# The lead of a hybrid decoder layer: rows normalized before they are turned, bias and norm weight taken into the modulation's dot products, all weight blocks split in two, and filler passes on TensorE

## The chip, the cores and the metric

One core of a Trainium2 chip runs one launch of the kernel. The metric is the device time of a launch in microseconds. The engines are named as the profile names them: PE is TensorE's matmul (PEld its weight load), DVE is VectorE, ACT is ScalarE, POOL is GpSimd, SP is SyncE, which issues nearly all the loads from memory.

## The reference, cut to what matters

One decoder layer on 256 tokens of width 1024 (FFN width 2816), in float32:

```python
def rmsnorm(x, g):
    return x * lax.rsqrt(jnp.mean(x * x, -1, keepdims=True) + EPS) * g

mod = silu(c) @ w_ada + b_ada                       # 9 rows of 1024
sh1, sc1, g1, sh2, sc2, g2, sh3, sc3, g3 = jnp.split(mod, 9, axis=-1)
u = rmsnorm(h, norm_ff1) * (1 + sc1) + sh1
h = h + 0.5 * g1 * ((silu(u @ w_gate) * (u @ w_up)) @ w_down)
u = rmsnorm(h, norm_mix) * (1 + sc2) + sh2
h = h + g2 * token_mixing(u, ...)
u = rmsnorm(h, norm_ff2) * (1 + sc3) + sh3
h = h + 0.5 * g3 * swiglu(u, ...)
return rmsnorm(h, norm_final)
```

The change touches only the start: the first two lines of the first FFN (its modulation, its norm, and the first 8 of its 22 gate and up column blocks).

## The kernel before, in words

Activations stand feature-major: a tile holds 128 features on the partitions and 256 tokens along the row, and the width of 1024 is 8 such blocks k = 0..7. Float32 weights are multiplied in three passes: ACT copies a block of weights to a rounded part (`hi`), DVE subtracts it from the original to get the rest (`lo`), the activations `u` are parted in the same way (`uh`, `ul`), and PE adds hi·uh, hi·ul and lo·uh, 128x128 weights against 128x256 activations each time.

The **lead** is the kernel's first stage. Its 8 PSUM banks hold gate and up of the FFN's column blocks f = 0..7, 16 results of 128x256, and k runs in the outer loop, so that PE can begin when the first eighth of the weights is there. For each k the stage needs: the two dot products that give scale and shift of this block (`lead_dot`, letter d: a row of `w_ada` for each of the 128 features times silu(c), with `accum_out`), the sums with bias and norm weight (`lead_mods`, m), the normed block (`lead_normed`, n: x times 1/rms, which PE has spread over all partitions into `rb`), the modulated block `u` (`lead_u`, u, on ACT), its parts `uh` (`lead_uh`, c, ACT) and `ul` (`lead_ul`, v, DVE), and the weights' hi (`lead_high`, h, ACT) and lo (`lead_low`, r, DVE), in two pieces i = 0, 1. Of the 16 weight blocks, 14 are split; two (`NATIVE`) are multiplied unsplit in float32 (`lead_native`, p). `lead_mm` (x) issues the passes of one piece.

What stands in which order is written by hand: the string `LEADING` lists these steps by letter, k and piece, and `InOrder` chains each instruction of DVE, ACT and PE behind the one recorded before it on its engine. An engine therefore issues in the order of the string, and waits where its next instruction has to wait. `LOADS` gives the order of the loads on SP (a for `w_ada`, l for the weights, each in two pieces); they go into 4 buffers `raw`, so that a load of block k waits until a buffer of block k-2 has been read.

Behind the lead, `LED` finishes its 8 banks (silu, product, split), then the loop over `work1` runs the other gate/up blocks and the down projection of the first FFN, with the remaining dot products of the modulation between them (`AdaQueue`), then token mixing, then the second FFN and the last norm.

`h`, the residual in feature-major order, is made at the start: PE transposes x through `ident` into 4 banks, ACT copies them to `h` (`take_in`).

Of the kernel before, what the change touches and what calls it, by code (L numbers as in the profile page):

```python
# [77 lines left out]
def hybrid_layer(ctx: ExitStack, tc: tile.TileContext, x, cols, ident_d, tri_d, mask_d, onehot_d,  # L78
                 relT, wlr, ada, lead, gu1, dn1, win, gv, mv, gbr, wout, gu2, dn2, out):
# [90 lines left out]
    def split(raw, lo, width=1024, later=False, gap=False):  # L170
# [124 lines left out]
    for s in (1, 4, 7):  # L295
# [44 lines left out]
    class AdaQueue:  # L340
# [255 lines left out]
    def lead_dot(k, i):  # L596

        lead_load_until(f"a{k}{i}")
        ada_dot(ada_raw[k], 0 if i else D, 0 if i else 1, k)

    def lead_mods(k):
        vec.scalar_tensor_tensor(mods[:, 1, k:k + 1], gemv[:, 1, k:k + 1], bada[:, 1, k:k + 1],
                                 colt[:, C_N1 + k:C_N1 + k + 1], op0=ALU.add, op1=ALU.mult)
        vec.tensor_tensor(out=mods[:, 0, k:k + 1], in0=gemv[:, 0, k:k + 1], in1=bada[:, 0, k:k + 1], op=ALU.add)


    def lead_normed(k):
        if k:
            vec.tensor_tensor(out=xn[:, k, :S], in0=h[:, k, :S], in1=lead_rb[0][:, :S], op=ALU.mult)
        else:  # L610
            vec.scalar_tensor_tensor(xn[:, 0, :S], h[:, 0, :S], mods[:, 1, 0:1], rb[:, :S], op0=ALU.mult, op1=ALU.mult)

    def lead_u(k):
        us[k] = row(tag="u", bufs=3)
        act.activation(us[k], xn[:, k, :S], AF.Identity, scale=mods[:, 1, k:k + 1] if k else 1.0, bias=mods[:, 0, k:k + 1])

    def lead_uh(k):
        if k:
            act.activation(uh[:, k, :S], us[k], AF.Copy)
        else:  # L620
            act.activation(uh[:, 0, :S], xn[:, 0, :S], AF.Identity, bias=mods[:, 0, 0:1])

    def lead_ul(k):
        if k:
            vec.tensor_tensor(out=ul[:, k, :S], in0=us[k], in1=uh[:, k, :S], op=ALU.subtract)
        else:
            vec.scalar_tensor_tensor(ul[:, 0, :S], xn[:, 0, :S], mods[:, 0, 0:1], uh[:, 0, :S], op0=ALU.add,
                                     op1=ALU.subtract)
# [10 lines left out]
    def lead_native(k):  # L639
        for i in range(NATIVE):  # L640
            b = lead_banks[i // 2]
            mm(b[:, i % 2 * S:(i % 2 + 1) * S], b, lead_raw[k][:, blk(i)], us[k], stop=(k == KD - 1))

    def lead_mm(k, w):
        def to(at):
            i = NATIVE + w * half + at
            return lead_banks[i // 2][:, i % 2 * S:(i % 2 + 1) * S], lead_banks[i // 2]

        if k or w:
            for at in range(half):  # L650
                mm3(*to(at), ws[k, w], blk(at), (uh[:, k, :S], ul[:, k, :S]), stop=(k == KD - 1))
        else:

            for part, rows in ((0, uh), (1, uh), (0, ul)):
                for at in range(half):
                    mm(*to(at), ws[0, 0][part][:, blk(at)], rows[:, 0, :S])

    def lead_rbs():
        act.activation(rbs, rb[:, :S], AF.Copy)
        lead_rb[0] = rbs  # L660
# [40 lines left out]
    warm_bank = bank()
    for _ in range(WARM):
        ten.transpose(warm_bank[:, :P], ident, ident)
    ada_dot(ada_raw[0], D, 1, 0)
    ada_dot(ada_raw[0], 0, 0, 0)
    rbs, lead_rb = row(tag="rbs", bufs=1), [rb]
# [19 lines left out]
    def mix_constants():  # L726
        ctri = load(tri_d, 1536)
# [505 lines left out]
def _packed(i):  # L1233
    w = {k: np.asarray(v) for k, v in i.items()}
    d = {}
    d["x"] = _c(w["x"][0])
    vec = [w["b_ada"][0], w["norm_ff1"][0], w["norm_mix"][0], w["norm_ff2"][0], w["norm_final"], w["c"][0],
# [6 lines left out]
    first = rows[:2].transpose(1, 2, 0, 3).reshape(KD, P, 2 * D)  # L1244
# [44 lines left out]
```

## Time and profile before

| | us |
|---|---|
| median of 3 runs | 572.95 (572.29 to 573.03) |
| the profiled execution, its own time | 572.64 |
| its span on the core | 570.9 |
| PE busy | 557.3 (98%) |
| DVE busy | 442.8 (78%) |
| ACT busy | 300.8 (53%) |
| DMA queue of SP, share of 16 engines | 67.6% |

The profile is one execution. The page's first part gives the busy time of each engine over the whole span; windows give the same for any stretch, with PE's granted clock (1.00 is the higher of its two levels, 0.50 the lower) and what the DMA engines moved. A timeline lists instructions by start and duration, with the idle time before one and what ended it in square brackets. Instructions of DVE and ACT overlap a little at their ends, so what one costs in a row of them is the distance between two starts, and not its duration.

### The profile page before, as it was taken

To read this page: it belongs to the slowest core of one execution; us is meant where nothing else is said; L and a number is where in the kernel's file an instruction comes from. 1 tells how busy PE (TensorE), PEld (TensorE's weight loads), DVE (VectorE), ACT (ScalarE), POOL (GpSimd) and SP (SyncE) were. 2 spreads that over 40 slices of the span, in tenths; PEclk is the share of its full clock that TensorE was granted. 3 is DMA by queue.
4 is the path that set the end of the run, shared out by engine and by line. 5 is a ranking of instruction groups with operands and counts; after the bars stand their busy time and mean duration, and the time that the engine had idled before them with its cause. 6 is when DMAs were issued, how large, how long until landed. Compare 5 with 4: busy or idle time off the path is not lost.

```text
span 570.9 us, 11312 instructions
## 1 busy us (share of the span) xinstructions
PE 557.3 (98%) x4711; PEld 550.1 (96%) x4711; DVE 442.8 (78%) x701; ACT 300.8 (53%) x480; POOL 10.8 (2%) x14
## 2 busy tenths in 40 slices
PE   4999999999999999999999999999999999999996
PEld 3999999999999999998999999999999999999995
DVE  4999887879887896899998979789874656665534
ACT  5455664352536577843764544576644454345424
POOL 0000000000000010000001000001000000000000
PEclk9999999999999999999999999999999999999999
DMA  8999689898989726544489776842796566775102
GB/s 311 357 409 394 255 314 383 302 359 325 325 313 338 242 75 249 193 140 157 130 307 365 287 265 251 309 152 84 284 342 205 195 212 205 254 266 180 67 1 75
DMA packets 23237, 140.95 MB, mean 247 GB/s; under 512 B 2781, under 2 KB 3346, under 8 KB 8850
## 3 DMA queue, kind: packets, MB, share of 16 engines
q1 hardware_dynamic: 22722, 139.37, 67.6%
q8 instruction: 37, 0.61, 0.4%
q0 software_dynamic: 176, 0.53, 0.3%
q10 hardware_dynamic: 288, 0.33, 0.2%
q14 instruction: 14, 0.11, 0.1%
HBM read 139.16 MB, written 1.05 MB: 246 GB/s over the span
## 4 chain that ended last, share of the span: by engine, by line
PE 61%; issue 32%; DVE 4%; DMA 2%; SPq 0%; POOL 0%; ACT 0%; POOLq 0%; DVEq 0%
PE b L103 61%; DMA raw<-in_lead 2%; DVE b L103 1%; DVE lo L103 1%; DVE s L103 1%; DVE raw L103 0%; POOL tiny L363 0%; ACT hi L103 0%; SPq L579 0%; SPq L276 0%; POOLq L1284 0%; DVEq L1284 0%; ACT ub L103 0%; SPq L273 0%; DVE tiny L103 0%
## 5 line engine op out<-in xcount | busy, mean ns | idle before, releaser
L103 PE MATMUL b<-ub,hi 128*128 128x256 f32 (+1 forms) x1888 | 329.3, 279 | 3.2 <-ACT ub L103 3.2
L103 PEld LDWEIGHTS b<-ub,hi 128*128 128x128 f32 x1888 | 286.6, 189 | 5.1 <-ACT ub L103 3.4
L103 DVE TENSOR_TENSOR lo<-raw,hi 128x1024 fp32r<-128x1024 f32 (+2 forms) x188 | 223.2, 1211 | 66.6 <-ACT hi L103 65.1
L103 PE MATMUL b<-ub,lo 128*128 128x256 f32 (+1 forms) x944 | 261.1, 278 | 0.0
L103 ACT ACTIVATE hi<-raw 128x1024 fp32r<-128x1024 f32 (+2 forms) x188 | 191.5, 1044 | 83.4 <-issue 34.4
L103 PEld LDWEIGHTS b<-ub,lo 128*128 128x128 f32 x944 | 177.6, 189 | 0.0
L103 PE MATMUL b<-s,hi 128*128 128x256 f32 x960 | 165.4, 277 | 0.0
L103 PEld LDWEIGHTS b<-s,hi 128*128 128x128 f32 x960 | 144.8, 188 | 0.0
L103 PE MATMUL b<-s,lo 128*128 128x256 f32 x480 | 132.7, 277 | 0.0
L103 PEld LDWEIGHTS b<-s,lo 128*128 128x128 f32 x480 | 90.1, 188 | 0.0
L103 DVE SCALAR_TENSOR_TENSOR raw<-raw,cact 128x1024 f32<-128x1024 f32 x72 | 85.0, 1219 | 2.5 <-DMA raw<-in_ada 2.2
L103 ACT ACTIVATE s<-m 128x256 fp32r<-128x256 f32 x52 | 21.4, 417 | 76.7 <-DVE m L103 76.7
L103 ACT ACTIVATE sg<-b 128x256 f32<-128x256 f32 x46 | 17.0, 379 | 44.9 <-PE b L103 42.9
L103 DVE TENSOR_TENSOR s<-m,s 128x256 fp32r<-128x256 f32 x52 | 21.8, 424 | 20.6 <-ACT s L103 20.5
L103 DVE TENSOR_TENSOR m<-sg,b 128x256 f32<-128x256 f32 x43 | 17.8, 416 | 12.5 <-ACT sg L103 12.2
L103 ACT ACTIVATE s<-b 128x256 f32<-128x256 f32 (+5 forms) x33 | 13.9, 469 | 22.0 <-PE b L103 19.6
L103 PE MATMUL b<-hi,ub 128*128 128x264 f32 (+1 forms) x96 | 21.8, 321 | 0.0
L103 PEld LDWEIGHTS b<-hi,ub 128*128 128x128 f32 x96 | 15.8, 188 | 1.2
L103 PE MATMUL b<-lo,ub 128*128 128x264 f32 (+1 forms) x48 | 15.4, 321 | 0.0
L103 DVE SCALAR_TENSOR_TENSOR b<-b,mods,b 128x256 f32<-128x256 f32 x25 | 11.0, 477 | 4.7 <-PE b L103 4.6
L363 POOL TENSOR_TENSOR tiny<-tiny,mhalf 128x2 f32<-128x2 f32 (+1 forms) x5 | 7.1, 1418 | 365.5 <-DVE tiny L103 365.5
L103 ACT ACTIVATE sq<-b 128x256 f32<-128x256 f32 x24 | 9.2, 407 | 5.6 <-DVE b L103 5.2
(122 smaller groups left out, 276.4 us busy)
## 6 DMA issues: line engine op xcount, KB each, us to landing
raw<-in_gu SPq DMA_DIRECT2D x35, 1024.0 KB, 5.3
raw<-in_ada SPq DMA_DIRECT2D x28, 1024.0 KB, 6.1
raw<-in_dn SPq DMA_DIRECT2D x21, 1024.0 KB, 4.9
raw<-in_win SPq DMA_DIRECT2D x12, 1024.0 KB, 6.4
raw<-in_ada SPq DMA_DIRECT2D x16, 512.0 KB, 7.4
raw<-in_gbr SPq DMA_DIRECT2D x8, 1024.0 KB, 7.2
raw<-in_lead SPq DMA_DIRECT2D x8, 576.0 KB, 6.3
raw<-in_wout SPq DMA_DIRECT2D x4, 1024.0 KB, 5.9
```

The costliest lines, as they stand in the source:

```text
L103: x = getattr(self.engine, op)(*args, **kw)
L363: nc.gpsimd.tensor_tensor(out=rs[:, :n], in0=ms[:, :n], in1=mhalf[:, :n], op=ALU.pow)
```

## The change

- **Rows.** The sum of squares of the second 128 tokens is shared between ACT and DVE. Then 1/rms scales the rows of x in place while they are token-major (`lead_scaled`, s, ACT, in four halves), PE transposes the scaled rows (`lead_turned`, t) and ACT copies the banks to `xn` (`lead_xn`, e). `lead_normed`, `rb` and `rbs` go, and so does `lead_rbs`.
- **Dot products.** A row of `w_ada` comes with two more columns, the bias and 1 (scale) or 0 (shift); `cact` has two columns of 1 behind silu(c); the scale's dot product is multiplied by the norm weight. So `gemv` holds norm weight times (1 + scale), and the shift, at once. `lead_mods` goes. The rows of these loads are 4104 bytes long and contiguous (`adal`), where they were 4096 of 8192.
- **Blocks.** All 16 weight blocks are split: two pieces of 1024 columns, and `lead_native` goes. The passes of a piece go over the banks in another order (`IN_TURN`). The first piece of k = 0 is split in two halves on ACT and DVE.
- **Order.** `LEADING` has `v` (ul) directly behind the dot products and in front of `r` (lo of piece 0).
- **Filler passes.** `keep_warm` has PE transpose `ident` into a spare bank: 22 passes after silu(c) has been turned, 8 and 7 between and behind the transposes of x (5 before).
- **Residual.** `h` is no longer made from x at the start but loaded from a second, feature-major copy `xT` in `mix_constants`, 1 MB on SP's queue.

```diff
-WARM = 5
+WARM = (22, 8, 7)
...
-LEADING = """h00 m0 n0 c0 r00 v0 u0 b t n1 h01 r01 h10 d10 d11 m1 u1 c1 r10 v1 n2 h11 r11 x00 x01 p0 h20 d20 d21 m2
-         u2 c2 r20 v2 n3 h21 r21 p1 x10 x11 h30 d30 d31 m3 u3 c3 r30 v3 n4 h31 r31 p2 x20 x21 h40
...
+LEADING = """u0 c0 h00 e1 v0 r00 h01 e2 e3 d10 r01 d11 h10 u1 c1 v1 r10 h11 r11 x00 x01 h20 d20 d21 u2 c2 v2 r20 h21 r21
+             x10 x11 h30 d30 d31 u3 c3 v3 r30 h31 r31 x20 x21 h40 d40 d41 u4 c4 v4 r40 h41 r41 x30 x31
...
+        parts = [(src, to_hi, to_lo)]
+        if pieces == 2:
+            parts = [(src[:, i], to_hi[:, i], to_lo[:, i]) for i in range(2)]
...
-    cact = cst.tile([P, D], F32, name="cact")
+    cact = cst.tile([P, D + 64], F32, name="cact")[:, :D + 2]
+    vec.memset(cact[:, D:], 1.0)
...
+    warm = bank()
+
+    def keep_warm(n):
+
+        for _ in range(n):
+            ten.transpose(warm[:, :P], ident, ident)
+
+    keep_warm(WARM[0])
...
-    vec.scalar_tensor_tensor(sq[1], xt[:, D:2 * D], 1.0, xt[:, D:2 * D], op0=ALU.mult, op1=ALU.mult,
-                             accum_out=ssq[:, 1:2])
+    act.activation(sq[1][:, 0:512], xt[:, D:D + 512], AF.Square, accum_out=ssq[:, 1:2])
+    vec.scalar_tensor_tensor(sq[1][:, 512:], xt[:, D + 512:2 * D], 1.0, xt[:, D + 512:2 * D], op0=ALU.mult,
+                             op1=ALU.mult, accum_out=ssq[:, 2:3])
+    vec.tensor_tensor(out=ssq[:, 1:2], in0=ssq[:, 1:2], in1=ssq[:, 2:3], op=ALU.add)
...
     def lead_dot(k, i):
 
         lead_load_until(f"a{k}{i}")
-        ada_dot(ada_raw[k], 0 if i else D, 0 if i else 1, k)
-
-    def lead_mods(k):
...
+        src = ada_raw[k][:, 2 * GV * i:2 * GV * i + D + 2]
+        vec.scalar_tensor_tensor(src, src, 1.0 if i else colt[:, C_N1 + k:C_N1 + k + 1], cact, op0=ALU.mult,
+                                 op1=ALU.mult, accum_out=gemv[:, 1 - i, k:k + 1])
 
     def lead_u(k):
         us[k] = row(tag="u", bufs=3)
-        act.activation(us[k], xn[:, k, :S], AF.Identity, scale=mods[:, 1, k:k + 1] if k else 1.0, bias=mods[:, 0, k:k + 1])
+        if k:
+            act.activation(us[k], xn[:, k, :S], AF.Identity, scale=gemv[:, 1, k:k + 1], bias=gemv[:, 0, k:k + 1])
+        else:
+            vec.tensor_scalar(us[0], xn[:, 0, :S], gemv[:, 1, 0:1], gemv[:, 0, 0:1], op0=ALU.mult, op1=ALU.add)
...
     def lead_high(k, i):
         lead_load_until(f"l{k}{i}")
-        ws[k, i], rests[k, i] = split(lead_raw[k], (NATIVE + i * half) * P, half * P, True)
+        ws[k, i], rests[k, i] = split(lead_raw[k], i * D, later=True, gap=True, pieces=1 if k or i else 2)
...
+        rows, both = (uh, ul), range(KD)
+        order = [(at, *p) for at in IN_TURN for p in ((0, 0), (0, 1), (1, 0))]
+        if k == 0:
+            halves = (both,) if w else (range(4), range(4, 8))
+            order = [(at, 0, r) for part in halves for r in (0, 1) for at in part] + [(at, 1, 0) for at in both]
...
-    rb, _ = spread(rs, range(2))
...
+    def lead_scaled(t, half):
+        sl = slice(t * D + half * 512, t * D + (half + 1) * 512)
+        act.activation(xt[:, sl], xt[:, sl], AF.Copy, scale=rs[:, t:t + 1])
...
+    lead_dot(0, 0)
+    lead_dot(0, 1)
+    play("s00 t00 s10 t10 s01 w1 e0 s11 t01 t11 w2", {
+        "s": lead_scaled, "t": lead_turned, "e": lead_xn, "w": lambda i: keep_warm(WARM[i])})
...
+        nc.sync.dma_start(h.rearrange("p k s -> p (k s)"), xT)
...
+    more = np.zeros((2, KD, P, 2), np.float32)
+    more[:, :, :, 0] = w["b_ada"][0].reshape(9, KD, P)[:2]
+    more[1, :, :, 1] = 1.0
+    d["adal"] = _c(np.concatenate([rows[:2], more], 3)[::-1].transpose(1, 0, 2, 3))
```

In the rows that follow, a name stands for a tile (out <- in, then the shape): `raw` with `gemv` is a dot product, `mods` a sum with bias, `lo` a weight rest, `ub` the parts of the activations (here `ul`), `b_12`/`b_9` is `xn`, `tiny` the sums of squares.

DVE, block k = 2, before: seven rows from the dot products on.

```order
L103 SCALAR_TENSOR_TENSOR raw_253,gemv<-raw_253,cact 128x1024 x2
L103 SCALAR_TENSOR_TENSOR mods<-gemv,bada,colt 128x1
L103 TENSOR_TENSOR mods<-gemv,bada 128x1
L103 TENSOR_TENSOR lo_259<-raw_256,hi_258 128x896
L103 TENSOR_TENSOR ub_137<-u_265,ub_137 128x256
L103 TENSOR_TENSOR b_12_136<-b_7_112,rbs_165 128x256
L103 TENSOR_TENSOR lo_273<-raw_256,hi_272 128x896
```

The same in the changed kernel, with the next block's first row:

```order
L101 SCALAR_TENSOR_TENSOR raw_285,gemv<-raw_285,colt,cact 128x1026
L101 SCALAR_TENSOR_TENSOR raw_285,gemv<-raw_285,cact 128x1026
L101 TENSOR_TENSOR ub_75<-u_295,ub_75 128x256
L101 TENSOR_TENSOR lo_291<-raw_288,hi_290 128x2x512
L101 TENSOR_TENSOR lo_302<-raw_288,hi_301 128x2x512
L101 SCALAR_TENSOR_TENSOR raw_353,gemv<-raw_353,colt,cact 128x1026
```

The two `mods` rows and the normed block are gone, and `ub` has moved from behind the first `lo` to in front of it.

DVE, blocks 0 and 1, before:

```order
L103 SCALAR_TENSOR_TENSOR raw_138,gemv<-raw_138,cact 128x1024 x2
L103 SCALAR_TENSOR_TENSOR mods<-gemv,bada,colt 128x1
L103 TENSOR_TENSOR mods<-gemv,bada 128x1
L103 SCALAR_TENSOR_TENSOR b_12_136<-b_7_112,mods,b_154 128x256
L103 TENSOR_TENSOR lo_175<-raw_141,hi_174 128x896
L103 SCALAR_TENSOR_TENSOR ub_137<-b_12_136,mods,ub_137 128x256
L103 TENSOR_TENSOR b_12_136<-b_7_112,rbs_165 128x256
L103 TENSOR_TENSOR lo_189<-raw_141,hi_188 128x896
L103 SCALAR_TENSOR_TENSOR raw_144,gemv<-raw_144,cact 128x1024 x2
L103 SCALAR_TENSOR_TENSOR mods<-gemv,bada,colt 128x1
L103 TENSOR_TENSOR mods<-gemv,bada 128x1
L103 TENSOR_TENSOR lo_193<-raw_147,hi_192 128x896
```

and in the changed kernel:

```order
L101 SCALAR_TENSOR_TENSOR raw_139,gemv<-raw_139,colt,cact 128x1026
L101 SCALAR_TENSOR_TENSOR raw_139,gemv<-raw_139,cact 128x1026
L101 TENSOR_SCALAR u_206<-b_9_138,gemv 128x256
L101 TENSOR_TENSOR ub_75<-u_206,ub_75 128x256
L101 TENSOR_TENSOR lo_210<-raw_142,hi_209 128x512 x2
L101 SCALAR_TENSOR_TENSOR raw_145,gemv<-raw_145,colt,cact 128x1026
L101 TENSOR_TENSOR lo_218<-raw_142,hi_217 128x2x512
L101 SCALAR_TENSOR_TENSOR raw_145,gemv<-raw_145,cact 128x1026
L101 TENSOR_TENSOR ub_75<-u_228,ub_75 128x256
L101 TENSOR_TENSOR lo_226<-raw_148,hi_225 128x2x512
L101 TENSOR_TENSOR lo_234<-raw_148,hi_233 128x2x512
```

The dot products of block 1 now stand on both sides of the last `lo` of block 0, and in block 1 too `ub` stands ahead of both `lo`.

PE at the start, before (`csil` is silu(c), `b_1_72` is x, `tiny` is 1/rms being spread; a row with `ident` alone is filler):

```order
L103 MATMUL b_95<-ident,csil 128x128 x4
L103 MATMUL b_96<-ident,csil 128x128 x4
L103 MATMUL b_113<-ident,b_1_72 128x128 x2
L103 MATMUL b_114<-ident,b_1_72 128x128 x2
L103 MATMUL b_115<-ident,b_1_72 128x128 x2
L103 MATMUL b_116<-ident,b_1_72 128x128 x2
L103 MATMUL b_113<-ident,b_1_72 128x128 x2
L103 MATMUL b_114<-ident,b_1_72 128x128 x2
L103 MATMUL b_115<-ident,b_1_72 128x128 x2
L103 MATMUL b_116<-ident,b_1_72 128x128 x2
L103 MATMUL b_154<-ident,tiny_152 128x128 x2
L103 MATMUL b_157<-ident 128x128 x5
```

and in the changed kernel:

```order
L101 MATMUL b_96<-ident,csil 128x128 x4
L101 MATMUL b_97<-ident,csil 128x128 x4
L101 MATMUL b_106<-ident 128x128 x22
L101 MATMUL b_155<-ident,b_1_72 128x128 x2
L101 MATMUL b_156<-ident,b_1_72 128x128 x2
L101 MATMUL b_155<-ident,b_1_72 128x128 x2
L101 MATMUL b_156<-ident,b_1_72 128x128 x2
L101 MATMUL b_106<-ident 128x128 x8
L101 MATMUL b_158<-ident,b_1_72 128x128 x2
L101 MATMUL b_159<-ident,b_1_72 128x128 x2
L101 MATMUL b_158<-ident,b_1_72 128x128 x2
L101 MATMUL b_159<-ident,b_1_72 128x128 x2
```

The transposes of x have moved behind 22 filler passes and wait for the scaled rows; 8 and (behind the last row shown) 7 more filler passes stand between them and the first weights.

## Rows read from the trace of the kernel before

**Rows 1.** The page's first part: busy time, share of the span, instructions.

```profile
PE 557.3 (98%) x4711; PEld 550.1 (96%) x4711; DVE 442.8 (78%) x701; ACT 300.8 (53%) x480; POOL 10.8 (2%) x14
```

**Rows 2.** Windows: us, PE, PEld, DVE, ACT, POOL busy, clock, DMA share, GB/s.

```profile
60.00:560.00 500.00, 499.83 (x4270) 494.61 (x4269) 389.08 (x595) 263.71 (x420) 9.10 (x7) 1.00 0.66 235
```

**Rows 3.** Chain that ended last, 0 to 70 us: start, us, what.

```profile
12.79 0.41 ACT ub L103
...
13.24 56.82 PE b L103 x455
```

**Rows 4.** Windows of PE alone: us, busy (records), granted clock, DMA share, GB/s.

```profile
6.60:7.10 0.50, 0.50 (x7) 1.00 0.93 254
10.00:13.20 3.20, 0.05 (x1) 1.00 1.02 415
13.50:16.50 3.00, 3.00 (x16) 0.50 1.03 418
```

**Rows 5.** Timeline of PE: start, us, line, operation, tiles, shape, count.

```profile
26.92 0.58 PE L103 MATMUL b<-ub,hi 128*128 128x256 f32 x2
...
55.06 0.58 PE L103 MATMUL b<-ub,hi 128*128 128x256 f32 x2
...
55.59 0.39 PE L103 MATMUL b<-ub,hi 128*128 128x256 f32 x2
...
59.67 0.39 PE L103 MATMUL b<-ub,hi 128*128 128x256 f32 x2
```

**Rows 6.** Timeline of DVE, block 2 of the lead.

```profile
21.77 1.22 DVE L103 SCALAR_TENSOR_TENSOR raw<-raw,cact 128x1024 f32<-128x1024 f32 x1
...
22.91 1.22 DVE L103 SCALAR_TENSOR_TENSOR raw<-raw,cact 128x1024 f32<-128x1024 f32 x1
24.06 0.08 DVE L103 DVE_READ_ACCUMULATOR raw<-raw,cact 128x1 f32 x1
...
24.19 0.15 DVE L103 TENSOR_TENSOR mods<-gemv,bada 128x1 f32<-128x1 f32 x1
24.26 1.08 DVE L103 TENSOR_TENSOR lo<-raw,hi 128x896 fp32r<-128x896 f32 x1
25.47 0.43 DVE L103 TENSOR_TENSOR ub<-u,ub 128x256 fp32r<-128x256 f32 x1
25.81 0.42 DVE L103 TENSOR_TENSOR b<-b,rbs 128x256 f32<-128x256 f32 x1
...
27.32 1.22 DVE L103 SCALAR_TENSOR_TENSOR raw<-raw,cact 128x1024 f32<-128x1024 f32 x1
```

**Rows 7.** Timeline of ACT, the same stretch.

```profile
24.38 0.60 ACT L103 ACTIVATE u<-b,mods 128x256 f32<-128x256 f32 x1 [0.66 <-DVE mods L103]
25.01 0.42 ACT L103 ACTIVATE ub<-u 128x256 fp32r<-128x256 f32 x1
```

**Rows 8.** Groups by form, DVE: busy us, mean ns of one, idle before.

```profile
L103 DVE TENSOR_TENSOR lo<-raw,hi 128x1024 fp32r<-128x1024 f32 x168 | 201.0, 1222 | 64.6 <-ACT hi L103 63.6 <-PE b L103 0.8
...
L103 DVE SCALAR_TENSOR_TENSOR b<-b,mods,b 128x256 f32<-128x256 f32 x25 | 11.0, 477 | 4.7 <-PE b L103 4.6
...
L103 DVE TENSOR_TENSOR s<-s,s 128x512 fp32r<-128x512 f32 x2 | 1.4, 692 | 1.4 <-ACT s L103 1.4
```

**Rows 9.** Groups by form, ACT.

```profile
L103 ACT ACTIVATE wide<-wide 128x512 f32<-128x512 f32 x2 | 1.3, 633 | 0.0
```

**Rows 10.** Timeline of DVE and ACT at the start of the lead.

```profile
10.39 1.23 DVE L103 SCALAR_TENSOR_TENSOR raw<-raw,cact 128x1024 f32<-128x1024 f32 x1
11.54 0.08 DVE L103 DVE_READ_ACCUMULATOR raw<-raw,cact 128x1 f32 x1
...
11.84 0.95 ACT L103 ACTIVATE hi<-raw 128x896 fp32r<-128x896 f32 x1 [2.96 <-DMA raw<-in_lead]
...
16.97 0.96 ACT L103 ACTIVATE hi<-raw 128x896 fp32r<-128x896 f32 x1 [1.79 <-DMA raw<-in_lead]
```

**Rows 11.** Timeline of DVE at the lead's end.

```profile
54.10 3.36 DVE L103 TENSOR_TENSOR lo<-raw,hi 128x896 fp32r<-128x896 f32 x3 [0.42 <-ACT hi L103]
```

More of the change, by code (lines that the diff above doesn't have):

```diff
@@ L168, in load, with split @@
         return t
-    def split(raw, lo, width=1024, later=False, gap=False):
+    def split(raw, lo, width=1024, later=False, gap=False, pieces=1):
         hi = wp.tile([P, 2 * GV], F32R, tag="hi", name=name("hi"), bufs=HL)
@@ L350, in step @@
                 s, q = self.todo.pop(0)
-                raw = load(ada[4 * s + q])
+                raw = load(ada[4 * (s - 2) + q])
                 ada_dot(raw, 0, s, 2 * q)
@@ L620, in lead_uh @@
         else:
-            act.activation(uh[:, 0, :S], xn[:, 0, :S], AF.Identity, bias=mods[:, 0, 0:1])
+            act.activation(uh[:, 0, :S], xn[:, 0, :S], AF.Identity, scale=gemv[:, 1, 0:1], bias=gemv[:, 0, 0:1])
     def lead_ul(k):
[L624 to L628, printed above, removed]
+        vec.tensor_tensor(out=ul[:, k, :S], in0=us[k], in1=uh[:, k, :S], op=ALU.subtract)
     rests = {}
@@ L633, in lead_high @@
         lead_load_until(f"l{k}{i}")
-        ws[k, i], rests[k, i] = split(lead_raw[k], (NATIVE + i * half) * P, half * P, True)
+        ws[k, i], rests[k, i] = split(lead_raw[k], i * D, later=True, gap=True, pieces=1 if k or i else 2)
     def lead_low(k, i):
         rests[k, i]()
[L639 to L642, printed above, removed]
     def lead_mm(k, w):
[L645 to L660, printed above, removed]
+        rows, both = (uh, ul), range(KD)
[3 more added lines that the diff above has]
+            order = [(at, 0, r) for part in halves for r in (0, 1) for at in part] + [(at, 1, 0) for at in both]
+        for at, part, r in order:
+            b = lead_banks[4 * w + at // 2]
+            mm(b[:, at % 2 * S:(at % 2 + 1) * S], b, ws[k, w][part][:, wblk(at)], rows[r][:, k, :S],
+               stop=(k == KD - 1 and part == 1))
     lead_load_until(to_load[2 * RAW - 1])
@@ L699, in hybrid_layer, with lead_turned, lead_xn @@
     rs = rstd(ssq, D, 2)
-    rb, _ = spread(rs, range(2))
[L701 to L706, printed above, removed]
+    turned_x = [bank(), bank()]
+    bank()
+    turned_x += [bank(), bank()]
+    def lead_scaled(t, half):
+        sl = slice(t * D + half * 512, t * D + (half + 1) * 512)
+        act.activation(xt[:, sl], xt[:, sl], AF.Copy, scale=rs[:, t:t + 1])
+    def lead_turned(t, half):
+        for k in range(4 * half, 4 * half + 4):
+            ten.transpose(turned_x[k // 2][:, blk(k % 2 * 2 + t)], xt[:, t * D + k * P:t * D + (k + 1) * P], ident)
+    def lead_xn(i):
+        act.activation(xn[:, 2 * i:2 * i + 2].rearrange("p k s -> p (k s)"), turned_x[i], AF.Copy)
+    lead_dot(0, 0)
+    lead_dot(0, 1)
+    play("s00 t00 s10 t10 s01 w1 e0 s11 t01 t11 w2", {
+        "s": lead_scaled, "t": lead_turned, "e": lead_xn, "w": lambda i: keep_warm(WARM[i])})
     lead_banks = [bank() for _ in range(LEAD)]
-    play(LEADING, {"d": lead_dot, "m": lead_mods, "n": lead_normed, "u": lead_u, "c": lead_uh, "v": lead_ul,
-                   "h": lead_high, "r": lead_low, "p": lead_native, "x": lead_mm, "b": lead_rbs, "t": lambda: take_in(3), "A": stream.more})
+    play(LEADING, {"d": lead_dot, "u": lead_u, "c": lead_uh, "v": lead_ul, "h": lead_high, "r": lead_low,
+                   "e": lead_xn, "x": lead_mm, "A": stream.more})
+    h = big()
     hid = Hidden()
```

57 lines of the change are left out of this document (19 added, 38 removed).

## The prediction

> **What bounds the kernel now.** I read the page's first part, then the windows, then the chain of the first 70 us. PE is busy for 557.3 of 570.9 us [rows 1], and from 60 to 560 us it is busy for 499.83 of 500 [rows 2]. So nothing behind the lead can give back time lost in the lead or swallow time won there: the prediction is the shift of the moment at which PE has done the lead's last pass. Before, that moment is 60.01: the chain is a wait for `uh`, which ACT finishes at 13.20, and then PE without a pause [rows 3]; the last group of three passes starts at 59.67, and such groups stand 0.34 apart (12 of them from 55.59 to 59.67) [rows 5]. PE pays 5.63 us for a block of the lead ((55.06 - 26.92)/5) [rows 5]. The second thing to see is DVE: its period per block is 5.55 us (21.77 to 27.32), nearly all filled [rows 6]. PE has only 0.08 us per block in hand over DVE, so the lead has two bounds that nearly tie, and an edit has to be costed on both.
>
> **PE's side of the change.** Each block loses two unsplit matmuls and gets two more groups of three. Now a block is 16 groups of 0.34, 5.44 us, against 5.63: 0.19 less per block, 1.5 us in all [rows 5]. Each pass is 0.113 us. At the start the wait for `uh` gets shorter: the last dot product is out at 11.62 [rows 10]; before, two sums, the normed block and ACT's pass followed, to 13.20 [rows 3]. Now `c0` on ACT follows at once, 0.60 long as `u` is with its two column operands [rows 7], so `uh` is there at 12.26. The first half of `hi` is there at 12.92 (below). Ahead of the first weights PE still has 4 transposes and 7 fillers, 11 records at 14 per us (7 in 0.5 us [rows 4]), 0.8 us behind the last scaled half of x, and that half stands ahead of `c0` on ACT: 11.7 + 0.8 = 12.5. So PE starts at 13.0, against 13.24. Before, the clock stood at 0.50 from 13.5 to 16.5 after PE had been idle from 10.0 to 13.2 [rows 4]; with the fillers there is no such pause. If DVE kept up, PE would run 384 passes from 13.0 on, 43.5 us, and end at 56.5, 3.5 us early. That is the most the change can bring.
>
> **DVE's side, term by term.** What is removed per block: two `mods` sums (0.20 from 24.06 + 0.08 to 24.34) and the normed block, 0.34 to 0.50 [rows 6]. What is added: 128 columns on each `lo`, so that both last 1.222 [rows 8] and start 1.15 apart, as the dot products do (22.91 to 24.06). What is moved is `ul`. Before, DVE did the first `lo` (24.26) while ACT made `u` and `uh` for it; the two took from 24.38 to 25.43, and `ul` began at 25.47 [rows 6, 7]. Now `ul` stands in front of that `lo`, directly behind the second dot product, and DVE, which issues in order, waits for ACT with both `lo` queued behind the wait. Both `lo` are what PE waits for: the third pass of a group needs the first of them. One period of DVE is then:
> - first dot product 1.15, plus 0.06 for its column operand (477 ns [rows 8] against 420 without one [rows 6]): 1.21;
> - second dot product and the reading of its sum, 1.15 + 0.08 = 1.23 [rows 6];
> - the way over ACT: 0.04 to the start of `u`, 0.63 to the start of `uh`, 0.42 for it, 0.04 back [rows 6, 7]: 1.13;
> - `ul` 0.34 (25.47 to 25.81) [rows 6];
> - two `lo`, 2 x 1.15 = 2.30.
>
> That is 6.21 us (6.15 if the column operand costs nothing), against 5.44 for PE. DVE becomes the bound of the lead; without the wait of 1.13 it would be 5.08, and PE would be the bound.
>
> **The end of the lead.** The start of DVE's chain: sum out at 11.62 [rows 10]; `c0` 11.66 to 12.26; `ul` of block 0 at 12.30, done with its slot at 12.64. ACT's first half of `hi` starts 0.63 behind `c0`, at 12.29, and lasts 0.63 [rows 9], to 12.92; two half `lo`, 0.69 long [rows 8] and 0.61 apart, end DVE's slot at 14.18. Block 1's first dot product needs its load: the weights of block 0 landed at 11.84 [rows 10], two pieces of together 0.98 MB follow in the queue, and at 415 GB/s [rows 4] they are there at 14.2. Take 14.25. Then 1.21 (dot product), 1.15 (the last `lo` of block 0), 1.23 (dot product), 1.13 (ACT), 0.34 (`ul`), 2.30 (both `lo`): block 2 starts at 21.61. For `u` of block 1 ACT must have its `hi`: that load landed at 16.97 [rows 10] and comes 64 KB earlier in the queue now, so it is no later than the sum at 17.84. Five periods of 6.21 bring block 7 to 52.66; its first `lo` is done 1.21 + 1.23 + 1.13 + 0.34 + 1.22 later, at 57.79. PE takes its third pass at 57.83 and has 46 passes from there, 5.21 us: 63.04. The shift is 63.04 - 60.01 = +3.0 us.
>
> PE itself is ready long before: at 18.4 it has done block 0 and then waits for block 1's `lo` until 20.5. So the saved passes, the earlier start and the clock are all paid back as waits, and a fall of the clock in that pause would be covered too: it cost 3.0 us at half speed before [rows 4], 1.5 us, and PE has 0.77 in hand per block from there on.
>
> **What is hidden.** The fillers and the 8 transposes lie in time in which PE waits anyway. The load of `xT`, 1.05 MB, is 2.5 us of the DMA engines at 415 GB/s [rows 4]; behind 60 us they are busy 0.66 of the time [rows 2], and it stands ahead of other loads on SP, so without that cover it costs up to 2.5 us once. `w_ada` and weights, 2.1 MB per 6.21 us, are 338 GB/s, under the 415 seen. Behind the lead DVE had its next `lo` done at 57.46 [rows 11], 2.55 us ahead of PE; now two more follow the lead's last one (58.9) and end at 61.2, 1.8 us ahead of PE's 63.04. Still ahead, so no further loss.
>
> The new load rows are 4104 bytes long. Before, the lead's loads had rows of 3584 to 4608 bytes, multiples of 512, and ran at 415 GB/s [rows 4]. The Trainium skill (DMA: Bandwidth & Descriptors, "How a descriptor splits into AXI transactions") has reads go in 256-byte transactions that start at a 256-byte boundary, so that a row which starts elsewhere fetches bytes it drops; no row here shows it. As an estimate from that page, up to 8 beats in 128 more, 6%, on four loads of 1.25 us each ahead of block 1's weights, it would add 0.3 us to the chain, and the sum would be +3.3.
>
> **Forecast.** The profiled execution took 572.64, 0.31 under the median of the runs. 572.64 + 3.0 = **575.7 us**. With the terms at their low ends (6.15, the start 0.5 earlier) it is +2.2, 574.8; with their high ends (loads 0.5 late, the median's 0.31, a clock that falls once and is not covered, 1.0) 577.5.
>
> **Rivals.**
> - *PE stays the bound, faster.* This decides as soon as DVE's period is under 5.44, that is, if the wait between the second dot product and `ul` is under 0.36 us and not 1.13. Then PE runs through from 13.0: 572.64 - 3.5 = 569.1, and 570.6 if the clock is low for the first 3.0 us all the same (1.5 us, as before [rows 4]). For it: DVE has less work than before (5.08 of 6.21). Against it: `u` and `uh` are two ACT passes of 0.60 and 0.42 in a row, both needed by `ul` [rows 7]. At 6.6 us PE ran at 14 transposes per us at a granted clock of 1.00 with nothing but transposes behind it [rows 4], so fillers seem to hold the clock. The Trainium skill (TensorE: Matmul & The Clock Gate, "Part 4: PE-mode transpose") says that transposes do not count as busy in the same way; by that rule this rival is 570.6, and not 569.1. Chance 0.10.
> - *More than DVE's wait: the clock or the loads.* If PE's pauses of 0.77 us per block let the clock fall again and again, a block takes up to 10.9 us at half speed, and even two falls of 3.0 us that are not covered cost 3 us more: 578.7. If `xT` is not hidden, 2.5 more: 578.2. Against it: before, the clock fell only behind 3.2 us without work [rows 4], four times such a pause. Chance 0.10.
> - *It does less than it says*: the wait is there but the start gains more than I count, or work behind the lead gives time back. The sum would be within 1.1 us: about 573. Rows 2 leave 0.17 us to give back. Chance 0.07.
>
> **How the numbers follow.** Forecast 0.73, with 574.8 to 577.5 as its own range. To 8 in 10 the range needs half of the two neighbours: 573.4 to 577.9. A measurement of this kernel tells about 0.2%, 1.1 us, from no change. Faster: 0.10 and a little of the third rival, 0.11. Same: 0.07. Slower: 0.82.
>
> **What would show it.** Right: in the lead DVE idles some 1.1 us per block ahead of `ub<-u,ub`, ended by ACT `ub`; its period is 6.2; PE waits about 0.8 us per block, ended by DVE `lo`, and its longest pause is in block 1; the clock is 1.00 at the first weights; work behind the lead begins near 63. Wrong: a period of DVE near 5.4 or less with no such idle time; PE without waits from 13 us on; a lead that ends before 60; waits of DVE for loads (`raw<-in_adal`) in place of ACT; PE waits behind 65 us.

## The result and the profile after

The changed kernel took 575.57 us (median of 4 runs, 575.14 to 576.67) against 572.62 (572.09 to 573.03). The ratio is 1.0055, 95% interval 1.0038 to 1.0072: slower by 2.95 us, where 575.7 was forecast. The mechanism that was forecast is in the trace. But the sum came out by luck too: two terms that the forecast did not have, +1.86 and -1.82 us, almost cancel.

The page's first part, after, against [rows 1]; columns are busy time, share of the span, instructions:

```profile
PE 558.8 (97%) x4757; PEld 551.0 (96%) x4757; DVE 439.3 (77%) x680; ACT 305.3 (53%) x485; POOL 10.8 (2%) x14
```

DVE has less work than before, and the kernel is slower. The timeline of DVE, after, block 2 of the lead (answers to [rows 6]; start, length, what; in brackets the idle time ahead and what ended it):

```profile
21.44 1.28 DVE L101 SCALAR_TENSOR_TENSOR raw<-raw,colt,cact 128x1026 f32<-128x1026 f32 x1
22.64 1.22 DVE L101 SCALAR_TENSOR_TENSOR raw<-raw,cact 128x1026 f32<-128x1026 f32 x1
23.79 0.08 DVE L101 DVE_READ_ACCUMULATOR raw<-raw,cact 128x1 f32 x1
25.00 0.42 DVE L101 TENSOR_TENSOR ub<-u,ub 128x256 fp32r<-128x256 f32 x1 [1.12 <-ACT ub L101]
25.34 2.35 DVE L101 TENSOR_TENSOR lo<-raw,hi 128x1024 fp32r<-128x1024 f32 x2
27.61 1.28 DVE L101 SCALAR_TENSOR_TENSOR raw<-raw,colt,cact 128x1026 f32<-128x1026 f32 x1
```

The period is 27.61 - 21.44 = 6.17 us (forecast 6.21, before 5.55), and 1.12 of it is the wait for ACT ahead of `ub<-u,ub`. Between the sum at 23.79 and the end of that wait ACT does this (answers to [rows 7]):

```profile
23.91 0.60 ACT L101 ACTIVATE u<-b,gemv 128x256 f32<-128x256 f32 x1 [0.58 <-DVE raw L101]
24.55 0.42 ACT L101 ACTIVATE ub<-u 128x256 fp32r<-128x256 f32 x1
```

The waits of the changed kernel, the first line from 12 to 63 us, the others of PE over the whole span (who waits, for whom, us in total, times, longest):

```profile
DVE ub L101 <- ACT ub L101: 8.5, 8, 1.1
...
PE b L101 <- DVE lo L101: 3.3, 7, 0.8
...
PE b L101 <- DMA relt<-in_relT: 1.9, 1, 1.9
```

So PE waits for `lo` in each of blocks 1 to 7; from start to start a block of the lead takes it the 6.17 us of DVE, 0.73 over its own 5.44. The third line is new, and not in the forecast. Four moments of PE give the balance. Its timeline, before, at the first pass on `s` (one unit of 48 passes, 5.44 us, behind the lead's end), at the matmul with `relt`, and at the last transposes of the program:

```profile
65.45 0.40 PE L103 MATMUL b<-s,hi 128*128 128x256 f32 x2
...
81.96 0.80 PE L103 MATMUL b<-wide,relt 32*4 32x384 f32 x2
...
563.56 1.94 PE L103 MATMUL b<-ident,b 128*128 128x128 f32 x16
```

The same three, after:

```profile
68.27 0.39 PE L101 MATMUL b<-s,hi 128*128 128x256 f32 x2
...
86.64 0.80 PE L101 MATMUL b<-wide,relt 32*4 32x384 f32 x2 [1.88 <-DMA relt<-in_relT]
...
566.42 1.94 PE L101 MATMUL b<-ident,b 128*128 128x128 f32 x16
```

The lead brings +2.82 (68.27 - 65.45; it ends at 62.83 instead of 60.01). From there to `relt` another +1.86 (86.64 - 81.96 = 4.68 in all). Then 1.82 comes back: from `relt` to the last transposes PE needs 479.78 us instead of 481.60. In all this is +2.86, as the span says (573.7 against 570.9). The middle and the last term are what the experiments had to explain, beside the first.

Where the `relt` term starts is seen on SP's queue. Before:

```profile
63.85 0.43 SPq L729 DMA_DIRECT2D mask<-in_mask  x1
...
70.63 0.41 SPq L729 DMA_DIRECT2D relt<-in_relT  x1
...
76.16 0.35 SPq L167 DMA_DIRECT2D raw<-in_tri  x1
```

After, where `xT` and `tri` stand ahead of the small loads and `tri` waits for a free `raw` buffer:

```profile
67.21 1.33 SPq L717 DMA_DIRECT2D b<-in_xT  x1
...
79.52 0.33 SPq L165 DMA_DIRECT2D raw<-in_tri  x1
...
80.84 0.42 SPq L720 DMA_DIRECT2D relt<-in_relT  x1
```

`relt` is issued 10.2 us later, with a lead that ends only 2.8 later, and lands when PE already waits for it.

### The profile page after: what moved, and what is told of

It is laid out like the page before. It is cut to its first block, busy times and chain, and to the rows that moved or that the text cites. A ratio compares the mean times of both kernels' runs of the same rounds, so it can differ in the third digit from the quotient of the medians.

```text
span 573.7 us, 11383 instructions
## 1 busy us (share of the span) xinstructions
PE 558.8 (97%) x4757; PEld 551.0 (96%) x4757; DVE 439.3 (77%) x680; ACT 305.3 (53%) x485; POOL 10.8 (2%) x14
## 4 chain that ended last, share of the span: by engine, by line
PE 52%; issue 33%; DVE 10%; ACT 2%; DMA 2%; POOL 0%; SPq 0%; DVEq 0%; POOLq 0%
PE b L101 52%; DVE lo L101 4%; DVE raw L101 3%; DVE b L101 1%; DVE s L101 1%; DMA relt<-in_relT 1%; DMA b<-in_x 1%; ACT u L101 1%; ACT ub L101 1%; ACT b L101 1%; POOL tiny L366 0%; SPq L720 0%; POOLq L1279 0%; DVEq L1279 0%; ACT hi L101 0%
## 5 line engine op out<-in xcount | busy, mean ns | idle before, releaser
L101 PE MATMUL b<-ub,lo 128*128 128x256 f32 (+1 forms) x960 | 264.0, 277 | 3.3 <-DVE lo L101 3.3
L101 DVE SCALAR_TENSOR_TENSOR raw<-raw,cact 128x1024 f32<-128x1024 f32 (+1 forms) x64 | 75.8, 1219 | 0.0
```

Source lines behind the costliest of these rows:

```text
L101: x = getattr(self.engine, op)(*args, **kw)
```

## Experiments

Times are medians; the runs of the kernel before beside each group gave 572.29 (first four), 572.55 (next four) and 572.23 us (last three).

**1. The one move, put into the kernel before.**

```diff
-h20 d20 d21 m2 u2 c2 r20 v2 n3 h21 r21
+h20 d20 d21 m2 u2 c2 v2 r20 n3 h21 r21
```

(and so in blocks 1 to 7)

> The kernel before with only the one move: in blocks 1 to 7 the low part of the rows ahead of the first lo on DVE (ub, lo, lo instead of lo, ub, lo). My theory: DVE then idles 1.1 us per block ahead of the low part, its period goes from 5.55 to about 6.2, and over 7 blocks the lead ends 3 to 4.5 us later than at 60.0; time 575.6 to 577.2. Rival (the change's loss is of its other parts: longer first stage, unaligned rows of 4104 bytes, xT): within 0.5 us of 572.6.

Measured: 576.5 us, ratio 1.0070 (1.0058 to 1.0082), +4.2. DVE's timeline of this kernel, block 2:

```profile
21.89 1.22 DVE L103 SCALAR_TENSOR_TENSOR raw<-raw,cact 128x1024 f32<-128x1024 f32 x1
...
25.59 0.43 DVE L103 TENSOR_TENSOR ub<-u,ub 128x256 fp32r<-128x256 f32 x1 [1.12 <-ACT ub L103]
...
28.27 1.22 DVE L103 SCALAR_TENSOR_TENSOR raw<-raw,cact 128x1024 f32<-128x1024 f32 x1
```

The same 1.12 us appear and the period is 6.38. Nothing else of the change is in this kernel, so the move alone is enough to make the lead late.

**2. The move taken back in the changed kernel.**

```diff
-u2 c2 v2 r20 h21 r21
+u2 c2 r20 v2 h21 r21
```

> The changed kernel with, in blocks 1 to 7, the first lo subtraction ahead of the low part of the rows again (DVE: lo, ub, lo instead of ub, lo, lo); all else as changed. My theory (DVE's wait for ACT's u and ub, 1.12 us per block, delays both lo): the wait goes, DVE's period falls from 6.17 us to about 5.2, under PE's 5.44, and PE sets the pace: 8 blocks of 5.44 from 13.1, so the lead ends near 57.0 instead of 62.7 and the time is about 570.0 us (the 1.9 us idle of PE at 84 us still there). Rival 1, the loads set the pace (2.10 MB per block; at the 350 GB/s of the changed kernel's first 60 us that is 6.0 us per block): ACT's hi waits for DMA in most blocks, lead end above 60, time 573.5 to 575. Rival 2, it is not DVE's order: no change, 575.5.

Measured: 573.7 us, ratio 1.0018 (1.0004 to 1.0031), with runs from 571.36 to 575.06: only 1.9 us less, not 5.5. The wait for `ub` is gone, but DVE's timeline of this kernel shows another:

```profile
37.10 0.42 DVE L101 TENSOR_TENSOR ub<-u,ub 128x256 fp32r<-128x256 f32 x1
38.05 1.22 DVE L101 TENSOR_TENSOR lo<-raw,hi 128x1024 fp32r<-128x1024 f32 x1 [0.52 <-ACT hi L101]
...
42.75 0.43 DVE L101 TENSOR_TENSOR ub<-u,ub 128x256 fp32r<-128x256 f32 x1
43.69 1.23 DVE L101 TENSOR_TENSOR lo<-raw,hi 128x1024 fp32r<-128x1024 f32 x1 [0.52 <-ACT hi L101]
```

ACT makes `u`, `ub`, and then the second `hi`; DVE now arrives at the second `lo` 0.52 us before that `hi` is done. The period is 43.69 - 38.05 = 5.64, still over PE's 5.44. The rival of the loads named 573.5 to 575, and the time lies in that range; but in this trace DVE waits for late weights only in block 2 (1.0 us), and kernel 4 below, with the same loads in its lead, is 4.0 us faster. PE reaches `s` at 65.42 (68.27 in the changed kernel), 2.85 earlier, with a first pass 0.5 later, since `x` landed later in this execution. So the move is worth some 3 us in the lead, and my 5.08 for DVE without its wait was short by half a microsecond. Part of the gain is lost again at `relt`: PE's row there and the windows around it (us, busy (records), granted clock, DMA share, GB/s):

```profile
83.93 0.80 PE L101 MATMUL b<-wide,relt 32*4 32x384 f32 x2 [2.03 <-DMA relt<-in_relT]
```

```profile
81.00:84.00 3.00, 0.97 (x9) 1.00 1.02 334
84.00:87.00 3.00, 3.00 (x14) 0.68 0.97 366
87.00:90.00 3.00, 3.00 (x22) 0.75 1.01 418
```

Behind this pause the granted clock was under 1.00 in the next two windows: the trace has it at 0.50, the lower level, from 85.11 to 88.52 us. In the changed kernel, behind its 1.88 us, it stayed at 1.00.

**3. The small constants ahead of `tri` and `xT`, all else as changed.**

```diff
-        nc.sync.dma_start(h.rearrange("p k s -> p (k s)"), xT)
-        ctri = load(tri_d, 1536)
         for to, src in ((mask, mask_d), (onehot, onehot_d), (relt, relT), (wlr_s, wlr)):
             nc.sync.dma_start(to, src)
+        ctri = load(tri_d, 1536)
+        nc.sync.dma_start(h.rearrange("p k s -> p (k s)"), xT)
```

> The changed kernel with the five loads of the constants in another order: mask, onehot, relt and wlr first, then tri, xT last (changed: xT, tri, mask, onehot, relt, wlr). Theory A (xT in front of the raw buffers' loads on SP's queue moved relt from 70.6 to 80.8 us, and PE stands at 84.6 for 1.88 us): the idle of PE at 84 us goes and the time falls by 1.9 us to 573.7. Theory B (the megabyte of xT itself is what delays everything, and its delay only shows elsewhere): another load lands late, the time stays within 0.7 us of 575.5.

Measured: 573.77 us, ratio 1.0024 (1.0015 to 1.0033), 1.8 less than the changed kernel. On SP `relt` is issued at 73.69, and PE's row of this kernel has no wait:

```profile
84.38 0.80 PE L101 MATMUL b<-wide,relt 32*4 32x384 f32 x2
```

Theory A holds. The megabyte of `xT` is still loaded, at 79.71, and costs nothing there: from `relt` to the last transposes PE needs 479.77 us, as in the changed kernel (479.78). So it was the order of the queue, not the bytes. The edit moves `xT` and `tri`, and in the kernel before `tri` was issued behind `relt`; which of the two held `relt` back was not separated.

**4. Both together.** Edits 2 and 3 in one kernel.

> The changed kernel with the first lo subtraction ahead of the rows' low part in blocks 1 to 7 (as lo_first) and the small constants loaded first, xT last (as small_first). If the two causes are separate, the gains add: lo_first's 1.9 us and small_first's 1.8 us, so 575.6 - 3.7 = 571.9 us. If the idle of PE at 82 us (2.3 us in lo_first, and the granted clock 0.83 in the 10 us around it) hid more of lo_first's gain, which moved the passes ahead of that idle 2.9 us forward, the time is 575.6 - 1.8 - 2.9 = 570.9 or less. If the two are one cause: 573.7.

Measured: 569.68 us, ratio 0.9949 (0.9936 to 0.9961), 2.9 faster than before and 5.9 faster than as changed. That is more than the sum of the two gains, 3.7. PE's timeline of it, at `s` and at `relt`, against 68.27 and 86.64 as changed:

```profile
64.63 0.39 PE L101 MATMUL b<-s,hi 128*128 128x256 f32 x2
...
81.04 0.48 PE L101 MATMUL b<-wide,relt 32*4 32x384 f32 x1
```

The lead is 3.64 earlier and the pause at `relt` is gone: 5.60 in all, and its span is 5.6 us shorter. So the two causes are separate, and in kernel 2 part of the first one's gain was hidden; in its one trace by the slow clock behind the longer pause, and by weights of block 2 that landed late (DVE waited 1.0 us for their `hi`, and PE passed `s` 0.8 later than here).

**5. The second term that was not foreseen: where tiles lie.** The change also takes the tile of the rows' parts (`ub`) ahead of the mid tiles, so that both lie at other addresses. That line was moved alone, first in the kernel before:

```diff
     for t in range(2):
         nc.sync.dma_start(xt[:, t * D:(t + 1) * D], x[blk(t)])
+    uh, ul = parts_tile()
...
     xn = big()
-    uh, ul = parts_tile()
```

> The kernel before with one line moved: the tile of the rows' two parts (ub, 20480 bytes per partition) is taken ahead of the mid tiles, as in the changed kernel, so that it and the mid tiles lie at other addresses of SBUF; no instruction is added, taken away or reordered on purpose. Theory A (in the trace of before some 740 passes behind the lead are 115 to 130 ns from start to start instead of 113.3, in the changed kernel 320, and the difference is one of placement): the slow passes fall to about 320 and the time by about 2.0 us to 570.6. Theory B (they come with the phase in which ACT's and DVE's instructions meet the passes): nothing changes, 572.6.

and then back, in the changed kernel (the reverse of this diff):

> The changed kernel with one line moved back: the tile of the rows' two parts is taken where the kernel before takes it, behind the mid tiles; no instruction is changed. Theory A (placement: the change won some 2 us behind the lead by moving this tile): the passes of 115 to 130 ns behind the lead rise from 324 to about 740 and the time by 1.2 (what the reverse move gave in medians) to 2.0 us, to 576.8 to 577.6. Theory B (the fewer slow passes come from something else in the change): unchanged, 575.5.

Measured: 571.05 us, ratio 0.9977 (0.9968 to 0.9986), for the kernel before; 579.1, ratio 1.0108 (1.0090 to 1.0126), for the changed one. The windows of PE from 400 to 550 us, in the order before, after, the kernel before with the tile early, the changed one with the tile late:

```profile
400.00:550.00 150.00, 150.00 (x1320) 1.00 0.60 210
```

```profile
400.00:550.00 150.00, 150.00 (x1326) 1.00 0.61 211
```

```profile
400.00:550.00 150.00, 150.00 (x1326) 1.00 0.59 206
```

```profile
400.00:550.00 150.00, 150.00 (x1320) 1.00 0.61 211
```

PE is busy all the time at full clock in all four, and does six more passes in 150 us wherever the tile is early, 0.45%. Between `relt` and the last transposes the two kernels with the early tile need 479.78 and 479.93 us, the two with the late one 481.60 and 481.73 (of the second of each pair: 81.22 to 561.15, and 86.28 to 568.01). With the traces of the other experiments, nine with the early tile need 479.77 to 479.94 us for this stretch, three with the late one 481.60 to 481.73 (the trace of experiment 2 is not among them, since its slow clock lies in the stretch). So theory A is shown for PE's pace in both directions, some 1.8 us. In the starts of single passes the late placement has some 740 and 840 passes of 115 to 130 ns behind 60 us, the early one 325 and 354; most others are 113.3. Which of the two tiles matters, and what it meets at its address, was not separated.

The times of the two kernels are less clean. The first gained 1.2 us of the 2.0 expected. In its profiled execution the span is 2.41 us shorter, but only 1.67 of this lie behind `relt`; most of the rest is in the lead, where PE's first passes begin at 12.76 us and not 13.24, and 0.113 us apart and not 0.213 as in the trace of before. The late kernel's 3.5 us over the changed one are more than that: its profiled execution, the fastest of six, is 1.6 over (577.10), and what the others lost no trace shows.

**6. The fillers.** The changed kernel without them:

```diff
-WARM = (22, 8, 7)
+WARM = (0, 0, 0)
```

> The changed kernel without the 37 filler transposes. Theory A (they hold the granted clock, but the lead waits for DVE, not for PE): PE idles up to 13.1 us and works at granted clock 0.5 for some 3 us behind it, block 0 ends near 20.2 us instead of 18.7, still ahead of the third pass of block 1 (20.4 in the changed kernel), so at most 0.5 us is lost: 575.5 to 576.1. Theory B (the clock's loss shows in full): 577. Theory C (transposes hold no clock, as in the one reading that they count as no activity): granted clock at 13 to 16 us and time both unchanged, 575.5.

Measured: 575.96 us, ratio 1.0060 (1.0037 to 1.0082), 0.4 over the changed kernel. PE's timeline of it:

```profile
10.26 3.95 PE L101 MATMUL b<-ident,b 128*128 128x128 f32 x16 [5.25 <-ACT b L101]
14.11 2.69 PE L101 MATMUL b<-ub,hi 128*128 128x256 f32 x16
```

Single transposes in this row start 0.213 us apart, and so do the first passes of the lead, 0.214, up to 15.1; with the fillers it is 0.109 and 0.113. So PE does run at half its pace without them, up to 1.0 us behind the lead's first pass, and block 0 lasts 6.17 us to the first pass of block 1 (14.11 to 20.28) where with them it is 5.72 (13.12 to 18.84). That half microsecond is covered, since block 1 waits for DVE anyway. What is not covered lies ahead of it: ACT's copy of the turned rows waits for the slow transposes, and DVE's `u` of block 0 for that copy (ACT and DVE without fillers, then DVE with them):

```profile
11.84 0.60 ACT L101 ACTIVATE b<-b 128x512 f32<-128x512 f32 x1 [0.41 <-PE b L101]
...
12.47 0.41 DVE L101 TENSOR_SCALAR u<-b,gemv 128x256 f32<-128x256 f32 x1 [0.88 <-ACT b L101]
...
11.30 0.41 DVE L101 TENSOR_SCALAR u<-b,gemv 128x256 f32<-128x256 f32 x1 [0.38 <-ACT b L101]
```

The wait is 0.50 us longer, at the head of DVE's chain, and that is about what the median lost; the other 0.67 us by which `u` is later in this trace were there before the wait. Theory A holds in the time and in the pace: 0.213 is also the distance of the passes in the kernel before while the granted clock stood at 0.50 [rows 4]. The window of this stretch prints 1.00 (windows of PE; us, busy, clock, DMA share, GB/s):

```profile
10.00:14.00 4.00, 3.72 (x16) 1.00 1.02 415
```

But that is not a reading. The clock records of this trace begin at 15.31 us, and a stretch without a record is printed as 1.00 (in the kernel before they begin at 6.65, in the changed one at 7.97). Theory C falls by the distances of the starts.

**7. Taking DVE's new wait away.** Three edits on kernel 4: both `hi` ahead of `u` in blocks 3 to 7; that without fillers; and, in place of it, the next block's first dot product put on DVE between `ul` and the second `lo`:

```diff
-h30 d30 d31 u3 c3 r30 v3 h31 r31
+h30 h31 d30 d31 u3 c3 r30 v3 r31
```

> As both, and in blocks 3 to 7 ACT makes both hi halves ahead of u and ub, so that the second lo no longer waits for its hi (0.53 us per block in lo_first, whose DVE period was 5.65). My theory: DVE's period would be 5.1 and PE's 5.44 is the longer: some 0.2 us less per block over 5 blocks than in both, about 1.0 us: 570.9 - 1.0 = 569.9, PE's first passes on s near 64.4 instead of 65.4. Rival (the loads are the limit: 2.10 MB per block at the 377 GB/s that lo_first moved from 5 to 50 us, its DMA engines busy all the time, is 5.57 us per block): gain below 0.5 us, and ACT's hi waits for DMA in every block.

> As hi_first without the 37 filler transposes. Theory A (the fillers hold the clock, and where PE sets the pace the clock's loss shows): granted clock 0.5 for some 3 us behind 13 us and 1.0 to 1.5 us slower than hi_first. Theory B (they hold nothing): no difference.

```diff
-h20 d20 d21 u2 c2 r20 v2 h21 r21 x10 x11 h30 d30 d31
+h20 d20 d21 u2 c2 r20 v2 h21 d30 r21 x10 x11 h30 d31
```

> As both, and on DVE the first dot of the next block stands between the low part and the second lo in blocks 2 to 6, so that DVE has work while ACT makes the second hi. Theory A (DVE's wait of 0.53 us per block is what holds the period at 5.65): DVE 5.1, PE's 5.44 sets the pace, 5 times 0.2 = 1.0 us less than both, 568.7. Theory B (the loads hold it as well, since a lead buffer comes free 1.2 us later): no gain or a loss, 569.5 to 571, and PE waits for DVE lo or ACT hi behind DMA.

Measured: 570.67 us, 0.9957 (0.9944 to 0.9971); 570.82, 0.9969 (0.9958 to 0.9980); 569.05, 0.9944 (0.9931 to 0.9958). The first is no gain over kernel 4, as its rival said. ACT's timeline of it shows why:

```profile
29.01 1.07 ACT L101 ACTIVATE hi<-raw 128x1024 fp32r<-128x1024 f32 x1 [2.21 <-DMA raw<-in_lead]
30.28 1.06 ACT L101 ACTIVATE hi<-raw 128x1024 fp32r<-128x1024 f32 x1 [0.20 <-DMA raw<-in_lead]
31.25 0.59 ACT L101 ACTIVATE u<-b,gemv 128x256 f32<-128x256 f32 x1
```

`u` could have started at 30.4, and now stands on ACT behind a `hi` that waits for its weights. PE pauses in block 3 for it. The 1.0 to 1.5 us that theory A of the second expected don't show. In the two traces they are covered: PE pauses in block 2 or 3 for `uh`, behind late loads, with the fillers or without.

The last one does what was asked of it up to block 6: from 25.33 to 52.25 no two starts on PE are over 0.13 us apart, so it runs at its own 5.44 per block. Then the loads catch it, as theory B has it; ACT in block 7:

```profile
50.36 1.06 ACT L101 ACTIVATE hi<-raw 128x1024 fp32r<-128x1024 f32 x1 [3.55 <-DMA raw<-in_lead]
```

It is the fastest median of all, 0.6 under kernel 4, and by their intervals the two can't be told apart.

**8. Rows of 4104 bytes.** Kernel 4 with the rows at multiples of 512 bytes in DRAM:

```diff
-    more = np.zeros((2, KD, P, 2), np.float32)
+    more = np.zeros((2, KD, P, 128), np.float32)
...
-adal[k, i])
+adal[k, i, :, :D + 2])
```

> As both, with the modulation's rows 4608 bytes apart in DRAM instead of 4104, so that each begins at a multiple of 512; the same 4104 bytes are loaded. Theory A (unaligned rows make these loads slower): the median from issue to landing of in_adal falls from near 7 us towards in_lead's 6, and the loads of 5 to 50 us carry more than both's; as they are busy all the time there, up to 0.5 us faster than 569.7. Theory B (the 4104 bytes cost what they move): GB/s and time unchanged, 569.7 within 0.4.

Measured: 569.53 us, ratio 0.9951 (0.9939 to 0.9963); kernel 4 had 569.68. The DMA issues from 5 to 50 us, first of kernel 4, then of this one (KB each, median us from issue to landing):

```profile
raw<-in_lead SPq DMA_DIRECT2D x14, 512.0 KB, 6.6
raw<-in_adal SPq DMA_DIRECT2D x13, 513.0 KB, 7.0
```

```profile
raw<-in_lead SPq DMA_DIRECT2D x14, 512.0 KB, 6.1
raw<-in_adal SPq DMA_DIRECT2D x13, 513.0 KB, 6.7
```

Both kinds of load land a little earlier, the one whose rows are as before by 0.5 us, the other by 0.3; 387 GB/s against 386. No price of the odd rows can be seen.

## Why the prediction was right, point by point

- **What bounds the kernel.** Right: time lost in the lead is lost at the end, and the lead has two bounds that nearly tie. The page alone would have said the opposite, since DVE's total falls by 3.5 us. That nothing behind the lead could give time back is wrong (below).
- **DVE's period.** Right term by term: 1.20 and 2.36 for the dot products and the way over ACT (forecast 1.21 and 1.23 + 1.13), 0.34, and 2.27 for both `lo` (2.30). 6.17 against 6.21.
- **The start.** The sums were out at 10.92, not 11.62, since the first rows had landed early; `u` of block 0 then had to wait for the turned rows until 11.30, and the chain met the forecast again: first pass of PE at 13.12 (13.0), block 1's first dot product at 14.13 (14.25), block 2's at 21.44 (21.61). Two deviations that cancelled.
- **The end of the lead.** 62.83 against 63.04, shift +2.82 against +3.03.
- **"Still ahead, so no further loss."** Wrong. I costed `xT` as 2.5 us of the DMA engines, and looked whether DVE's next `lo` was early enough. I didn't follow each small load that is issued behind it on SP up to the instruction that needs it. It cost 1.86 us (experiment 3), and it is the sign "PE waits behind 65 us" that I had listed as wrong. The second rival had a price for an `xT` that is not hidden, 2.5 us; the loss came, but by the queue and not by the bytes.
- **A term that is missing.** PE's pace behind the lead: -1.82 us by the place of a tile. I read from 499.83 busy us of 500 [rows 2] that work there could give back 0.17 at most. But a busy share says nothing of pace: PE was busy all the time before and after, and its passes came closer together. By the traces the time would have been near 577.4 with the `relt` term alone, near 573.7 with this one alone, both near the ends of the range. As measured, experiment 3 has the second at 573.77, but the first, with the tile late (experiment 5), at 579.1, over the range. That the sum came out at 575.57 is luck in these two terms.
- **The first rival's price, 569.1.** Its premise was that without the 1.13 DVE needs 5.08. Experiment 2 found 5.64, as the same two ACT instructions then delay the second `hi`. Experiment 4 reached 569.68, but with the 1.82 of the placement in it.
- **The fillers.** That PE would be at its full pace at the first weights is right (row below, the windows of PE after). That a loss would be covered is right for the passes of block 0, but not for the transposes ahead of them (0.50 us, experiment 6). My 14 transposes per us from [rows 4] were misread: seven lie in that half microsecond, each 0.27 us long, but from start to start they are 0.109 apart, 9 per us. So the 11 passes ahead of the first weights took 1.1 us and not 0.8, and the first pass on weights, at 13.12, follows directly on the last filler; DVE's chain hid this. In the trace of the kernel before, with nothing but transposes on PE, these start 0.213 apart up to 6.66 us and 0.109 apart from 6.77 on, and the clock records begin at 6.65 with 1.00; where the fillers were left out, transposes and passes took longer. The Trainium skill's rule of transposes (TensorE: Matmul & The Clock Gate, "Part 4: PE-mode transpose"), by which they don't count as busy in the same way, does not agree with these rows: in this kernel transposes brought PE to its full pace and kept it there.

```profile
14.00:16.00 2.00, 2.00 (x20) 1.00 1.03 344
```

- **The unaligned rows.** My estimate of 0.3 us, worked out from the Trainium skill (DMA: Bandwidth & Descriptors, "How a descriptor splits into AXI transactions"), was not in the forecast, and experiment 8 shows none of it: 569.53 and 569.68.

## What to carry to other kernels

Where two engines nearly tie, cost the order and not the work: one instruction moved ahead of the two that the next engine waits for cost 4.2 us by itself (experiment 1), and the change as a whole lost time though DVE had less to do. When such a wait is taken away, work the period out again with every other wait, for the next one may stand half a microsecond behind. When a load is put in a queue, follow the small loads behind it to the instruction that needs them, and read the pace of an engine from the starts of its passes, since a busy share of 100% hides it. When a forecast comes true, still balance the trace at three or four moments, since here two errors of 1.8 us hid each other.

## What was not expected of the hardware

- The place of a tile in SBUF changed PE's pace by 0.45% at full granted clock with no wait in the trace: 1320 or 1326 passes in 150 us, in four kernels, some 1.8 us in all.
- Without fillers PE's transposes started 0.213 us apart instead of 0.109, as the passes did in the kernel before at a granted clock of 0.50 [rows 4]. The trace without fillers has no clock record ahead of 15.31 us, and its windows print 1.00 there. The starts were the safer sign.
- Transposes alone brought PE to its full pace: in the kernel before at 6.66 us, in the changed one among the fillers at 7.97, from 0.213 to 0.109 us from start to start.
- A pause of PE of 2.03 us was followed by granted clocks of 0.68 and 0.75 in two windows of 3 us, one of 1.88 us in the changed kernel by 1.00.
